# Weight blocks in tiles of a low and a high half, sums stored and loaded as such, and 45 ring tiles

## The chip, the core and the metric

The kernel runs on one core of a Trainium2 chip. The metric is the device time of one execution in microseconds; the time of a version is the median of its runs. The engines are PE (matmuls; PEld is its weight load), DVE (vector work), ACT (activations and casts), POOL and SP (here mostly the issuing of DMAs).

## The reference, cut to what matters

2112 tokens (2048 of a prompt, 64 of a sample) go through one layer with 1024 channels, in fp32:

```python
h = rms_norm(x, g_pre)
vA, bA, cA, zA, q, f, iv, zB, gA, gB = split_cols(h @ w_in)
u = cA * vA
yA = (silu(zA) * bA * causal_conv3(u_ext, conv_w)) @ w_a_out
fg = lb + (1 - lb) * sigmoid(f)
S_new, o = hgrn2_scan(S0, silu(q) * K_B ** -0.5, 1 - fg, iv, log(fg))
o = o * rsqrt(mean(o * o) + EPS)
yB = (o * g_onorm * silu(zB)) @ w_b_out
out = (sigmoid(gA) * yA + sigmoid(gB) * yB) @ w_o
x = x + rms_norm(out, g_post)
gate = sigmoid(rms_norm(x, g_ple) @ w_ple_gate)
x = x + (p @ w_ple_proj) * gate
```

The outputs are x, the last rows of u and the states S_new.

## The kernel before

**Numbers.** A product of fp32 matrices is made of three matmuls: each operand is split into a high half (a cast) and a low half (the rest), and high by high, high by low and low by high are added up in PSUM. A weight block is 128 x 512 (four k of 128); splitting it costs a cast on ACT and a subtraction on DVE (`split`, L207). The low half is kept in DRAM (`lows`, tiles named low), so that a later block of tokens loads it instead.

**Stages.** Three blocks of 768, 704 and 640 tokens go one after the other through these stages: path_b (gates and the eight heads of the scan), path_a (the convolution's products), the merge (W_A, W_B), the output product (W_O), a norm, and the last gate (W_G). A block's norm and the first seven groups of the next block's gates run together.

**sgroup.** The products with w_in run as groups of seven products instead of eight, each of 4 k x 3 matmuls with the width of half a block (384, 352 or 320). Four of the seven take sums or differences of weight blocks (S1 to S4). The first block of tokens makes them (`combined`, `total`) and stores each (DRAM tiles S1 to S4, 256 KB) and its low half (256 KB). Later blocks load both and cast the first (L237). One step of other work is placed behind each product (`hook`; `spread_out` hands out the steps).

**Sums for the other weights.** In the merge of block 1, W_A and W_B run as plain products (`gemm`; the first two j together in `gemm_late`, which takes one k last), while `prepare_sums` makes the sums that blocks 2 and 3 will use (`in_turn`): eight groups of four blocks, loaded on POOL's queue into ring tiles, added and split on ACT and DVE, stored on POOL's queue. It goes on by one group behind W_A's j = 2, 4, 6 and W_B's j = 0, 2, 4, 6, 7. The sums for W_O and W_G are made in path_a of blocks 2 and 3, a whole group behind each j from 3 on.

**Tiles.** Weight blocks go through pools of raw (5), hi (4), lo (4) and s (3) tiles of 2 KB in each partition. Rows of tokens, up to 768 wide, lie in the ring: 47 tiles of one tag. While block 1's W_G runs, 28 of them hold the operands of block 2 and 16 hold W_G's own operand h2. Its results go through ACT (sigmoid) into hf tiles, of which there are nine, and are multiplied by p and added to x; p and x of each j are reloaded into ring tiles on POOL's queue (`reload`, L1107; `final_gate`, L1257 to L1260). Five PSUM banks hold the results of such products.

**Order.** Each engine works through its instructions in the order in which they were laid down; a scheduler lays them down when the program is built. An instruction that waits for a semaphore holds up all behind it on its engine, and a DMA is issued from its engine's queue in the same way.

Of the kernel before, what the change touches and what calls it, by code (L numbers as in the profile page):

```python
# [18 lines left out]
P = 128  # L19
# [4 lines left out]
CH = 64  # L24
# [15 lines left out]
RING = 47  # L40
# [43 lines left out]
def hybrid_step(  # L84
# [56 lines left out]
    def rt(n=None, dt=F32):  # L141
        return ring.tile([P, BMAX + 4], dt, tag="r", name=nm("r"))[:, : n or wide[0]]
# [71 lines left out]

    def load_raw(src):
        raw = wp.tile([P, 4, P], F32, tag="raw", name=nm("raw"), bufs=5)
        SP.dma_start(raw, src)
        return raw

    lows, turn = {}, [0]  # L220

    def low_tile():

        turn[0] += 1
        if turn[0] % 7 in (1, 3, 5):
            return sum_tile(F32R)
        return wp.tile([P, 4, P], F32R, tag="lo", name=nm("lo"))

    def sum_tile(dt=F32):
        return wp.tile([P, 4, P], dt, tag="s", name=nm("s"), bufs=3)  # L230

    def split_w(raw, key=None, queue=SP):

        hi = wp.tile([P, 4, P], F32R, tag="hi", name=nm("hi"))
        if key in lows:
            lo = low_tile()
            A.copy(hi, raw)  # L237
            SP.dma_start(lo.bitcast(F32), lows[key])
            return hi, lo
        lo = wp.tile([P, 4, P], F32R, tag="lo", name=nm("lo"))  # L240
        split(raw, hi, lo)
        if key is not None:
            lows[key] = dram.tile([P, 4, P], F32, tag=f"lo{key}", name=nm("low"), bufs=1)
            queue.dma_start(lows[key], lo.bitcast(F32))
        return hi, lo

    def load_w(idx, anew=False):

        parts = []
        for half_ in range(2):  # L250
            raw = load_raw(w_blk[idx, half_])
            with tc.high_priority():
                unread = W_A <= idx < W_O and (idx % KB < KH or half_ == 0)
                parts.append(split_w(raw, None if anew or unread else (idx, half_)))
# [37 lines left out]
    def keep_sum(name, i1, s, queue):  # L292

        sums.setdefault(i1, {})[name] = dram.tile([P, 4, P], F32, tag=f"{name}_{i1}", name=nm(name), bufs=1)
        queue.dma_start(sums[i1][name], s)
        return split_w(s, (i1, name), queue)

    def kept_w(i1, i2, name, anew=False):

        keys = dict(A11=(i1, 0), A12=(i1, 1), A22=(i2, 1))  # L300
        if name in keys:
            return split_w(load_raw(w_blk[keys[name]]), None if anew else keys[name])
        return split_w(load_raw(sums[i1][name]), (i1, name))

    def combined(i1, i2, first):

        queue = SP if first else G
        with tc.high_priority():
            if not first and i1 in sums:
                return {n: kept_w(i1, i2, n) for _, n, _, _, _ in PRODUCTS}  # L310
            a11, a21, a22, a12 = (load_raw(w_blk[i, h]) for i, h in ((i1, 0), (i2, 0), (i2, 1), (i1, 1)))
# [16 lines left out]
    def prepare_sums(firsts, ahead):  # L328
# [4 lines left out]
        def tile_of(dt=F32):  # L333
            return rt(4 * P, dt).rearrange("p (k c) -> p k c", c=P)

        def load(i1, i2):
            out = [tile_of() for _ in range(4)]
# [4 lines left out]
        def keep(name, i1, s):  # L342
            sums.setdefault(i1, {})[name] = dram.tile([P, 4, P], F32, tag=f"{name}_{i1}", name=nm(name), bufs=1)
            lows[i1, name] = dram.tile([P, 4, P], F32, tag=f"lo{name}_{i1}", name=nm("low"), bufs=1)
# [7 lines left out]
        for n, (i1, _) in enumerate(groups):  # L352
# [15 lines left out]
    def sgroup(i1, i2, hc, sink, first, mid=None, by_k=False):  # L368
# [5 lines left out]
        def product(n, ks):  # L374
# [3 lines left out]
            hi, lo = w[block]  # L378
# [52 lines left out]
    def plain_group(i1, i2, hs, sink, raws=None, between=None):  # L431
# [14 lines left out]
        def add(c, ks):  # L446
            for k in ks:
                hi, lo = w[c, k // KH]
# [1082 lines left out]
```

## Time and profile before

| | us |
|---|---|
| median of 3 runs (2616.1 to 2618.68) | 2617.19 |
| profiled execution | 2618.3 |
| its span | 2616.6 |
| PE busy | 2584.3 |
| DVE busy | 1648.8 |
| ACT busy | 1525.9 |
| POOL busy | 376.6 |
| loads of raw tiles from S, 256 KB each | 408 |

The span is the time from the first to the last instruction in the profile. Busy times count matmuls, vector and activation work, not the issuing of DMAs or waits. A group's row gives its busy time, the mean of one instruction in ns, the idle time of its engine just before, and what ended that time. The DMA list gives for each kind of transfer its number, its size and the median time from issue to landing.

### The profile page before, as it was taken

Reading aid. Unit: us, or ns where it says so; the run is one execution under the profiler, and the core shown is the slowest. Engines: PE = TensorE matmul, PEld = TensorE weight load, DVE = VectorE, ACT = ScalarE, POOL = GpSimd, SP = SyncE. Lnnn points to the kernel's source line nnn. Section 1 sums busy time; section 2 is a strip of 40 time slices with the busy share of each in tenths; the row PEclk is TensorE's granted clock in tenths of the full one; section 3 lists DMA queues with packets and bytes.
Section 4 is the critical chain, followed back from the end, with each engine's and each line's share of the span. In section 5 each row is a group of like instructions: output and inputs, shape, how many; then the busy total and the mean of one; then the engine's idle time right before and its main releaser. Section 6 shows DMA issues by size and latency. Waiting matters only on the chain.

```text
span 2616.6 us, 47076 instructions
## 1 busy us (share of the span) xinstructions
PE 2584.3 (99%) x16432; PEld 2564.4 (98%) x16432; DVE 1648.8 (63%) x3165; ACT 1525.9 (58%) x2908; POOL 376.6 (14%) x698
## 2 busy tenths in 40 slices
PE   8999999999999999999999999999999999999999
PEld 8999999999999999999999999999999999999999
DVE  8687788788757655445554557845344444568776
ACT  6666576554433564567775546546677755556746
POOL 1000000110144021210011221002100000211110
PEclk9999999999999999999999999999999999999999
DMA  7677677788788698876768998859977779999977
GB/s 274 220 262 265 232 247 263 274 302 268 267 330 286 233 379 284 279 242 223 229 224 296 364 381 304 305 167 377 366 252 244 245 254 332 381 335 359 344 264 264
DMA packets 362095, 747.01 MB, mean 285 GB/s; under 512 B 44513, under 2 KB 49153, under 8 KB 361857
## 3 DMA queue, kind: packets, MB, share of 16 engines
q1 hardware_dynamic: 319680, 579.81, 64.2%
q0 software_dynamic: 41888, 164.15, 17.2%
q8 instruction: 129, 2.11, 0.3%
q14 instruction: 110, 0.89, 0.1%
q10 hardware_dynamic: 288, 0.05, 0.0%
HBM read 532.26 MB, written 211.57 MB: 284 GB/s over the span
## 4 chain that ended last, share of the span: by engine, by line
PE 82%; DMA 5%; ACT 4%; DVE 3%; issue 2%; POOL 1%; ACTq 0%; POOLq 0%; SPq 0%; DVEq 0%
PE pg L382 16%; PE pg L383 16%; PE pg L384 16%; PE pg L551 5%; PE pg L550 5%; PE pg L549 5%; PE pg L516 4%; PE pg L517 4%; PE pg L518 3%; DMA raw<-S 2%; DMA r<-w_blk 1%; PE pa L984 1%; PE pa L1020 1%; PE pa L970 1%; ACT hi L237 1%
## 5 line engine op out<-in xcount | busy, mean ns | idle before, releaser
L382 PE MATMUL pg<-r,hi 128*128 128x320 f32 (+2 forms) x3304 | 1087.5, 329 | 5.5 <-DVE r L429 3.8
L383 PE MATMUL pg<-r,hi 128*128 128x320 f32 (+2 forms) x3304 | 1069.3, 324 | 0.0
L384 PE MATMUL pg<-r,lo 128*128 128x384 f32 (+2 forms) x2356 | 766.9, 326 | 4.1 <-DMA lo<-low 4.1
L237 ACT CAST hi<-raw 128x512 fp32r<-128x512 f32 x720 | 442.9, 619 | 465.5 <-PE pg L383 137.2
L382 PEld LDWEIGHTS pg<-r,hi 128*128 128x128 f32 x3304 | 622.6, 188 | 7.9 <-issue 4.7
L383 PEld LDWEIGHTS pg<-r,hi 128*128 128x128 f32 x3304 | 622.7, 188 | 0.2 <-DVE r L207 0.2
L384 PEld LDWEIGHTS pg<-r,lo 128*128 128x128 f32 x2356 | 443.2, 188 | 5.1 <-DMA lo<-low 5.1
L384 PE MATMUL pg<-r,s 128*128 128x352 f32 (+1 forms) x948 | 299.3, 316 | 1.0 <-DMA s<-low 1.0
L549 PE MATMUL pg<-r,hi 128*128 128x384 f32 (+1 forms) x768 | 256.1, 334 | 1.6 <-ACT r L207 1.6
L550 PE MATMUL pg<-r,hi 128*128 128x384 f32 (+1 forms) x768 | 256.1, 334 | 0.1
L207 ACT CAST hi<-raw 128x512 fp32r<-128x512 f32 x218 | 134.7, 620 | 178.2 <-PE pg L550 57.9
L207 DVE TENSOR_TENSOR r<-r,r 128x320 fp32r<-128x320 f32 (+7 forms) x298 | 182.0, 633 | 64.9 <-ACT r L207 63.9
L551 PE MATMUL pg<-r,lo 128*128 128x384 f32 (+1 forms) x656 | 219.9, 335 | 0.0
L517 PE MATMUL pg<-r,hi 128*128 128x320 f32 (+1 forms) x672 | 211.1, 316 | 0.2 <-DVE r L207 0.2
L516 PE MATMUL pg<-r,hi 128*128 128x320 f32 (+1 forms) x672 | 206.0, 316 | 0.9 <-ACT r L207 0.8
L207 DVE TENSOR_TENSOR lo<-raw,hi 128x512 fp32r<-128x512 f32 x218 | 149.3, 686 | 63.1 <-ACT hi L207 60.4
L207 ACT CAST r<-r 128x320 fp32r<-128x320 f32 (+7 forms) x298 | 161.0, 576 | 46.0 <-DVE r L715 12.7
L207 ACT CAST hi<-s 128x512 fp32r<-128x512 f32 x160 | 98.0, 618 | 145.7 <-PE pg L383 130.8
L384 PEld LDWEIGHTS pg<-r,s 128*128 128x128 f32 x948 | 178.5, 188 | 1.8 <-DMA s<-low 1.8
L396 ACT COPY hf<-pg 128x352 f32<-128x352 f32 (+2 forms) x354 | 156.7, 444 | 3.8 <-PE pg L384 3.6
L207 DVE TENSOR_TENSOR lo<-s,hi 128x512 fp32r<-128x512 f32 x160 | 110.1, 689 | 68.9 <-ACT hi L207 67.3
L549 PEld LDWEIGHTS pg<-r,hi 128*128 128x128 f32 x768 | 144.8, 189 | 2.2 <-ACT r L207 2.2
(365 smaller groups left out, 4097.7 us busy)
## 6 DMA issues: line engine op xcount, KB each, us to landing
raw<-w_blk SPq DMA_DIRECT2D x570, 256.0 KB, 4.2
lo<-low SPq DMA_DIRECT2D x411, 256.0 KB, 4.6
raw<-S SPq DMA_DIRECT2D x408, 256.0 KB, 4.4
low<-lo SPq DMA_DIRECT2D x314, 256.0 KB, 3.5
s<-low SPq DMA_DIRECT2D x309, 256.0 KB, 4.5
S<-s SPq DMA_DIRECT2D x152, 256.0 KB, 3.2
r<-w_blk POOLq DMA_DIRECT2D x64, 256.0 KB, 6.8
S<-r POOLq DMA_DIRECT2D x64, 256.0 KB, 5.8
```

Source lines behind the costliest of these rows:

```text
L207: return A.copy(hi, src).ins, V.tensor_tensor(lo, src, hi.bitcast(F32), ALU.subtract).ins
L237: A.copy(hi, raw)
L382: add(hi[:, k, :], xhi, start=start and k == 0, stop=False)
L383: add(hi[:, k, :], xlo, start=False, stop=False)
L384: last[0] = add(lo[:, k, :], xhi, start=False, stop=k == KH - 1).ins
L396: copied = A.copy(got[n], ps[bank])
L516: add(hi[:, k, :], xhi, start=start and k == 0, stop=False)
L517: add(hi[:, k, :], xlo, start=False, stop=False)
L518: last[0] = add(lo[:, k, :], xhi, start=False, stop=k == KH - 1).ins
L549: T.matmul(ps, hi[:, k % 4, :], xhi[:, c], start=k == ks[0], stop=False)
L550: T.matmul(ps, hi[:, k % 4, :], xlo[:, c], start=False, stop=False)
L551: last[0] = T.matmul(ps, lo[:, k % 4, :], xhi[:, c], start=False, stop=k == ks[-1]).ins
```

## The change

- A weight block lies in one tile of two halves, low first (tag w, 7 of them), which takes the place of the hi and lo tiles and, for loaded sums, of the raw tile.
- A sum is stored as one such tile (512 KB) and loaded as one, with no cast. Raw weight blocks are still loaded, cast, and completed by a load of the low half.
- The raw tag has 6 tiles, and its tiles also take the sums of the first block and, in `prepare_sums` during the merge of block 1, the high and low halves of each sum: eight to a group, where four s tiles held the low halves.
- `prepare_sums` makes S3 before S1. For W_O and W_G each group is cut into four pieces, placed behind the products of path_a's groups by way of hooks.
- `gemm_late` goes through the k in a circle behind the late one: from 4 on for block 2's W_O.
- The last block's heads get one empty hook more, the norm's plan has one step more before each spread of the root mean squares.
- The ring has 45 tiles of 768 + 2 columns instead of 47 of 768 + 4; the small tags qc, one and ms have one tile less each.

```diff
-RING = 47
+RING = 45
+WEIGHTS = 7
+RAWS = 6
...
-        return ring.tile([P, BMAX + 4], dt, tag="r", name=nm("r"))[:, : n or wide[0]]
+        return ring.tile([P, BMAX + 2], dt, tag="r", name=nm("r"))[:, : n or wide[0]]
...
+    def raw_tile(dt=F32):
+        return wp.tile([P, 4, P], dt, tag="raw", name=nm("raw"), bufs=RAWS)
+
+    def both():
+        return wp.tile([P, 2, 4, P], F32R, tag="w", name=nm("w"), bufs=WEIGHTS)
...
+    def get_w(src, key=None):
+        raw = load_raw(src)
+        if key not in lows:
+            return split_w(raw, key)
+        t = both()
+        A.copy(t[:, 1], raw)
+        SP.dma_start(t[:, 0].bitcast(F32), lows[key])
+        return t
...
     def kept_w(i1, i2, name, anew=False):
         keys = dict(A11=(i1, 0), A12=(i1, 1), A22=(i2, 1))
         if name in keys:
-            return split_w(load_raw(w_blk[keys[name]]), None if anew else keys[name])
-        return split_w(load_raw(sums[i1][name]), (i1, name))
+            return get_w(w_blk[keys[name]], None if anew else keys[name])
+        t = both()
+        SP.dma_start(t.bitcast(F32), sums[i1][name])
+        return t
...
             def total(name, x, y, op):
-                s = sum_tile()
+                s = raw_tile()
                 V.tensor_tensor(s, x, y, op)
-                out[name] = keep_sum(name, i1, s, queue)
+                out[name] = split_w(s)
+                queue.dma_start(sum_home(name, i1), out[name].bitcast(F32))
                 return s
...
         def keep(name, i1, s):
-            G.dma_start(sums[i1][name], s)
-            lo = sum_tile(F32R) if ahead else tile_of(F32R)
-            split(s, lo, lo)
-            G.dma_start(lows[i1, name], lo.bitcast(F32))
+            home = sum_home(name, i1)
+            hi, lo = (raw_tile(F32R) if ahead else blocks_of(F32R) for _ in range(2))
+            split(s, hi, lo)
+            G.dma_start(home[:, 1], hi.bitcast(F32))
+            G.dma_start(home[:, 0], lo.bitcast(F32))
...
             V.tensor_tensor(a22, a21, a22, ALU.add)
-            keep("S1", i1, a22)
             V.tensor_tensor(a21, a11, a21, ALU.subtract)
+            if not ahead:
+                yield
             keep("S3", i1, a21)
             V.tensor_tensor(a11, a22, a11, ALU.subtract)
+            if not ahead:
+                yield
+            keep("S1", i1, a22)
+            V.tensor_tensor(a12, a12, a11, ALU.subtract)
+            if not ahead:
+                yield
             keep("S2", i1, a11)
-            V.tensor_tensor(a12, a12, a11, ALU.subtract)
             keep("S4", i1, a12)
...
-        ks = [k for k in range(KB) if k != late] + [late]
+        ks = [(late + 1 + k) % KB for k in range(KB)]
...
-            hooks.extend([None] * 3 if first and hd == 0 else [])
+            hooks.extend([None] * (3 if first and hd == 0 else int(bl["last"] and len(attn) == 2)))
...
-                if j >= 3:
+                if j == 3:
                     next(sums_, None)
+                elif j > 3 and not first:
+                    hooks.extend([partial(next, sums_, None), None, None] * 4)
...
-            spread_out((norm, (0, 1, 0, 1) + (0, 1, 0) * KB + (0, 1, 0, 1) + (0, 1) * KB))
+            spread_out((norm, (0, 1, 0, 0, 1) + (0, 1, 0) * (KB - 1) + (0, 1) + (0, 1, 0, 0, 1) + (0, 1) * KB))
```

Three places of the built order. First DVE in the merge of block 1, behind W_B's j = 2. Its two result banks are pg_2345 and pg_2346 before, pg_1897 and pg_1898 now; the r tiles are the group's blocks and sums, the s and raw tiles the low halves of S1 (before) and S3 (now). Before:

```order
L356 TENSOR_TENSOR r_2322_9424<-r_2321_9423,r_2322_9424 128x512 [waits DMASW1_49,DMASW0_49]
L358 TENSOR_TENSOR r_2321_9423<-r_2320_9422,r_2321_9423 128x512 [waits DMASW7_49,DMASW3_49,DVE_49]
L207 TENSOR_TENSOR lo_2382_9662<-raw_2380_9659,hi_2381_9661 128x512 [waits DMAHW5_49,PE_49,Activation_49]
L1139 TENSOR_TENSOR r_2336_9462<-pg_2345_9483,r_2336_9462 128x384 [waits DMASW3_49]
L1139 TENSOR_TENSOR r_2336_9462<-pg_2346_9508,r_2336_9462 128x384
L207 TENSOR_TENSOR s_2356_9554<-r_2322_9424,s_2356_9554 128x512 [waits DMASW2_49,Activation_49]
```

Now:

```order
L359 TENSOR_TENSOR r_1876_8826<-r_1875_8825,r_1876_8826 128x512 [waits DMASW1_49,DMASW0_49]
L360 TENSOR_TENSOR r_1875_8825<-r_1874_8824,r_1875_8825 128x512 [waits DMASW7_49,DVE_49]
L1148 TENSOR_TENSOR r_1890_8864<-pg_1897_8883,r_1890_8864 128x384 [waits DMASW3_49,PE_49]
L1148 TENSOR_TENSOR r_1890_8864<-pg_1898_8908,r_1890_8864 128x384 [waits PE_49]
L209 TENSOR_TENSOR raw_1908_8954<-r_1875_8825,raw_1907_8953 128x512 [waits DMASW4_49,Activation_49]
```

The first low half of the group stands behind the product's two result banks in both. What moved is its tile: it was an s tile, it is a raw tile now.

Second SP's queue at the same place, with the loads of the raw tiles for W_B's j = 3 (raw_2366 and raw_2369 before, raw_1918 and raw_1920 now). Before:

```order
L217 DMA raw_2366_9582<-w_blk 128x512 [waits DMAHW3_49,DVE_49]
L217 DMA raw_2369_9588<-w_blk 128x512 [waits DMAHW5_49,DVE_49]
L217 DMA raw_2377_9653<-w_blk 128x512 [waits DMAHW6_49,DMAHW4_49,DVE_49]
L217 DMA raw_2380_9659<-w_blk 128x512 [waits DMAHW0_49,DVE_49]
L217 DMA raw_2405_9766<-w_blk 128x512 [waits DMAHW1_49,DVE_49]
```

Now:

```order
L226 DMA raw_1895_8878<-w_blk 128x512 [waits DMASW6_49,DMAHW1_49,DMASW2_49,DVE_49]
L226 DMA raw_1918_8982<-w_blk 128x512 [waits DMAHW2_49,DMASW7_49,DMAHW5_49,DMASW4_49,DVE_49]
L226 DMA raw_1920_8987<-w_blk 128x512 [waits DMASW5_49,DMASW4_49,DVE_49]
L226 DMA raw_1927_9051<-w_blk 128x512 [waits DMAHW4_49,DMAHW2_49,DVE_49]
L226 DMA raw_1929_9056<-w_blk 128x512 [waits DMAHW6_49,DMASW6_49,DMASW5_49]
```

DMASW semaphores belong to POOL's DMAs, DMAHW to SP's. The loads waited for SP's own DMAs and for DVE; now they wait for DMAs of POOL as well. DMASW7 at raw_1918 is the store of raw_1908, the tile whose place it takes.

Third POOL's queue at block 1's W_G, with the reloads of p and x for j = 0 and 1 (r_2903, r_2904, r_2915, r_2918 before; r_2352, r_2353, r_2362, r_2365 now). Before:

```order
L1107 DMA r_2903_11978<-p_32_175 128x768 [waits DMASW7_49,DMASW3_49,DVE_49]
L1107 DMA r_2904_11980<-x_2802_11593 128x768 [waits DMASW4_49,DMASW1_49]
L1107 DMA r_2915_12048<-p_39_203 128x768 [waits DMASW5_49,DMASW2_49]
L1260 DMA y_fm<-r_2903_11978 128x768 [waits DMASW6_49,DVE_49]
L1107 DMA r_2918_12058<-x_2834_11679 128x768 [waits DMASW4_49]
L1107 DMA r_2929_12126<-p_46_231 128x768 [waits DMASW6_49,DMASW0_49]
```

Now, from the reload of x of j = 0 on (that of p stands six rows ahead and waits for no matmul):

```order
L1116 DMA r_2353_11221<-x_2274_10887 128x768 [waits DMASW1_49,PE_49]
L1116 DMA r_2362_11287<-p_39_203 128x768 [waits PE_49]
L1116 DMA r_2365_11297<-x_2296_10954 128x768 [waits DMASW3_49,PE_49]
L237 DMA low_2468_11871<-w_2467_11868 128x512 [waits DMASW4_49,DVE_49]
L1269 DMA y_fm<-r_2352_11219 128x768 [waits DMASW5_49,DVE_49]
L321 DMA S4_2471_11878<-w_2470_11875 128x1024 [waits DMASW6_49,DVE_49]
L1116 DMA r_2374_11363<-p_46_231 128x768 [waits DMASW7_49,PE_49]
L1269 DMA y_fm<-r_2362_11287 128x768 [waits DMASW0_49,DVE_49]
```

The reloads waited for other DMAs and for DVE. Now all but the first wait for PE: the tiles that they go into are those of W_G's operand, and r_2353 takes the place of a tile that the last of the sixteen products reads.

More of the change, by code (lines that the diff above doesn't have):

```diff
@@ L250, in load_w @@
         for half_ in range(2):
[L251 removed]
             with tc.high_priority():
                 unread = W_A <= idx < W_O and (idx % KB < KH or half_ == 0)
[L254 removed]
+                parts.append(get_w(w_blk[idx, half_], None if anew or unread else (idx, half_)))
         return parts
@@ L290, in hybrid_step, with sum_home @@
     sums = {}
[L292 to L296, printed above, removed]
+    def sum_home(name, i1):
+        home = dram.tile([P, 2, 4, P], F32, tag=f"{name}_{i1}", name=nm(name), bufs=1)
+        sums.setdefault(i1, {})[name] = home
+        return home
     def kept_w(i1, i2, name, anew=False):
@@ L310, in combined @@
                 return {n: kept_w(i1, i2, n) for _, n, _, _, _ in PRODUCTS}
+            queue = SP if first else G
             a11, a21, a22, a12 = (load_raw(w_blk[i, h]) for i, h in ((i1, 0), (i2, 0), (i2, 1), (i1, 1)))
@@ L936, in tile3 @@
             if nt == 1:
-                return small.tile([P, 1, P], F32, tag="one", name=nm("one"), bufs=5)
+                return small.tile([P, 1, P], F32, tag="one", name=nm("one"), bufs=4)
             return cols3(rt(nt * P), nt)
```

54 lines of the change are left out of this document (19 added, 35 removed).

## The prediction

> **What bounds the kernel now.** First the page's busy times, then the windows of 100 us, then what the matmul engine (PE) waits for, last the prices of the steps that the change puts in a chain.
>
> ```profile
> PE 2584.3 (99%) x16432; PEld 2564.4 (98%) x16432; DVE 1648.8 (63%) x3165; ACT 1525.9 (58%) x2908; POOL 376.6 (14%) x698
> ```
>
> PE is the bound: 2616.6 us of span less 2584.3 leave 32.3 us of idle time. Everything that the change takes from ACT lies under PE. So only two things count: which of these 32.3 us go, and which new ones come.
>
> ```profile
> 0.00:100.00 100.00, 91.10 (x510) 88.65 (x511) 76.71 (x139) 64.44 (x117) 14.06 (x29) 1.00 0.73 261
> 900.00:1000.00 100.00, 97.21 (x603) 95.49 (x602) 56.72 (x86) 63.45 (x116) 18.80 (x32) 1.00 0.96 349
> 1800.00:1900.00 100.00, 97.59 (x662) 96.82 (x660) 40.13 (x74) 63.10 (x118) 14.68 (x26) 0.98 1.01 377
> 2200.00:2300.00 100.00, 95.55 (x635) 94.38 (x635) 51.83 (x89) 50.62 (x101) 22.93 (x47) 0.98 1.02 379
> 750.00:800.00 50.00, 50.00 (x288) 50.00 (x287) 29.13 (x46) 14.91 (x25) 14.06 (x27) 1.00 0.67 243
> 1050.00:1100.00 50.00, 50.00 (x301) 50.00 (x300) 23.02 (x41) 24.85 (x42) 10.26 (x19) 1.00 0.77 272
> ```
>
> Columns: window, sum, PE, weight loads, DVE, ACT, POOL, PE clock, DMA share, GB/s. The first 100 us (8.9 idle) are not touched. Losses stand where DMA is full (0.96 to 1.02). The last two rows are the ones to keep: the merge of block 1 (W_A, W_B) and the end of its W_G have no idle time at all, and the change rebuilds the buffers just there.
>
> ```profile
> PE pg L384 <- DMA lo<-low: 4.1, 3, 2.2
> PE pg L382 <- DVE r L429: 3.8, 4, 1.8
> PE pa L953 <- DVE r L429: 2.0, 7, 0.3
> PE pa L624 <- POOL cols L613: 1.8, 6, 0.5
> PE pg L549 <- ACT r L207: 1.6, 2, 1.2
> PE pg L518 <- DMA lo<-low: 1.0, 1, 1.0
> PE pg L384 <- DMA s<-low: 1.0, 2, 0.5
> L382 PE MATMUL pg<-r,hi 128*128 128x320 f32 (+2 forms) x3304 | 1087.5, 329 | 5.5 <-DVE r L429 3.8 <-ACT hf L396 0.9 <-ACT hi L237 0.7
> 1701.50:1704.90 3.40, 3.40 (x13) 3.15 (x12) 2.56 (x6) 0.98 (x2) 0.00 (x0) 0.50 0.11 42
> 1803.90:1807.30 3.40, 3.40 (x15) 3.40 (x14) 1.83 (x3) 2.90 (x5) 0.54 (x1) 0.50 1.04 414
> ```
>
> The waits (total us, times, longest) give 15.3 us, L382's two smaller ones 1.6. The last two rows are the clock after W_O's stall and after one at 1803: 0.50 for 3.4 us, so 1.7 us more each. With a third in the window from 2200 (its mean clock is 0.98, too) that makes 5.1. At stake: 15.3 + 1.6 + 5.1 = 22.0 us.
>
> **What it removes.** 408 casts of loaded sums go from ACT:
>
> ```profile
> L237 ACT CAST hi<-raw 128x512 fp32r<-128x512 f32 x720 | 442.9, 619 | 465.5 <-PE pg L383 137.2 <-issue 66.0 <-DMA raw<-S 54.1
> L356 DVE TENSOR_TENSOR r<-r,r 128x512 f32<-128x512 f32 x16 | 11.0, 690 | 53.2 <-DMA r<-w_blk 53.2
> ```
>
> 408 x 0.619 = 252 us of ACT work, worth on PE only the 0.7 behind L237 and what ACT held up. Term by term: W_O of block 2 starts at k=4 with weights ahead, so its 1.6 and its dip of 1.7 go. The seven transposes (L953) get one more product between them and DVE: 2.0 goes. The pieces take L356's wait for a block (53.2 us on 10 occasions) out of the way of bank c's sum (L429): of L382's 5.5 I take 4.6, and one dip of 1.7. The bytes stay the same, in half as many loads, so of the 6.1 of waits for low halves I take 3.5, and half a dip, 0.9. Of L624's 1.8 the extra hook takes 0.8. Sum: 1.6 + 1.7 + 2.0 + 4.6 + 1.7 + 3.5 + 0.9 + 0.8 = 16.8. Bounds: 22.0 if all goes; 8.0 if only W_O (3.3), the transposes (2.0) and half of L382 (2.7) do.
>
> **What it adds in the merge of block 1.** The high and low halves of each prepared sum now lie in the raw tiles, which the weights are loaded into. A weight load must wait until a sum's store has landed, and that sum's split stands on DVE behind L1148 (L1139 before), which needs the matmuls just done (the DVE rows in the section on the change). W_B's j=3 (the rows shown), its j=7 and W_O begin behind such a chain, and nothing else is queued on PE. Prices:
>
> ```profile
> raw<-w_blk SPq DMA_DIRECT2D x570, 256.0 KB, 4.2
> S<-s SPq DMA_DIRECT2D x152, 256.0 KB, 3.2
> S<-r POOLq DMA_DIRECT2D x64, 256.0 KB, 5.8
> low<-lo POOLq DMA_DIRECT2D x8, 256.0 KB, 4.0
> raw<-w_ple SPq DMA_DIRECT2D x8, 128.0 KB, 2.8
> r<-w_blk POOLq DMA_DIRECT2D x64, 256.0 KB, 6.8
> L1139 DVE TENSOR_TENSOR r<-pg,r 128x384 f32<-128x384 f32 x16 | 8.7, 552 | 2.5 <-DMA r<-g__1389_5594 1.6 <-PE pg L551 0.9
> L207 DVE TENSOR_TENSOR lo<-raw,hi 128x512 fp32r<-128x512 f32 x218 | 149.3, 686 | 63.1 <-ACT hi L207 60.4 <-DMA low<-lo 1.2 <-ACT r L207 0.9
> L207 ACT CAST hi<-raw 128x512 fp32r<-128x512 f32 x218 | 134.7, 620 | 178.2 <-PE pg L550 57.9 <-PE pg L383 47.9 <-issue 38.3
> 1059.69 0.34 PE L549 MATMUL pg<-r,hi 128*128 128x384 f32 x1
> 1060.21 0.34 PE L549 MATMUL pg<-r,hi 128*128 128x384 f32 x1
> ```
>
> The chain at j=3: 0.55 (L1139) + 0.69 (sum's low) + a store from POOL of 4.9 (between 4.0 and 5.8) + a load of 4.2 + a cast of 0.62 + part of the next split, 0.35, + five hand-overs of some 0.1 = 11.8, taken as 11.5. Bounds: 8 with landings of 3.2 and 2.8, 14 with a store of 5.8 and a load that shares the queue with four block loads (6.8). Queued behind on SP are the three other weight loads of j=3 and j=4, and W_O's chain is the same: 11.5 (8 to 14). At j=7 the split waits for j=5's end, and j=6 covers 48 matmuls of 0.175 (0.52 for three, last two rows) = 8.4: 11.7 - 8.4 = 3.3 (0 to 5.6). At W_A's j=3 the store is queued on POOL behind eight loads, not behind PE: 2 (0 to 6).
>
> [...]
>
> **What 45 ring tiles add.** While W_G of block 1 runs, the next block's operands hold 28 tiles and h2 holds 16: 44. Of 47, three were left for the reloads of p and x; of 45, one is. So x of j=0, p and x of j=1 (the POOL rows in the section on the change) wait until the last of W_G's 16 gemms gives back h2's tiles. ACT can take nine results into hf tiles and two more from j=0's, the last five stay in PSUM, and path_b's first bank needs one of them.
>
> ```profile
> r<-p POOLq DMA_DIRECT2D x8, 384.0 KB, 5.3
> r<-x POOLq DMA_DIRECT2D x8, 384.0 KB, 5.6
> L1258 DVE TENSOR_TENSOR r<-r,hf 128x384 f32<-128x384 f32 (+1 forms) x32 | 17.2, 538 | 36.9 <-DMA r<-p 24.4 <-ACT hf L1257 12.3
> L1259 DVE TENSOR_TENSOR r<-r,r 128x768 f32<-128x768 f32 (+1 forms) x16 | 14.8, 922 | 0.3
> L1257 ACT ACTIVATE hf<-pg 128x384 f32<-128x384 f32 (+1 forms) x32 | 15.2, 475 | 40.6 <-PE pg L551 40.6
> 1085.08 0.33 PE L383 MATMUL pg<-r,hi 128*128 128x352 f32 x1
> 1085.57 0.32 PE L383 MATMUL pg<-r,hi 128*128 128x352 f32 x1
> ```
>
> From the last gemm's start: x issued at 0.2, landed at 5.8; add 0.9, product with the gate 0.55, sigmoid 0.5: 7.8 us. The gemm lasts 24 x 0.175 = 4.2, so PE waits 3.6. The third bank needs p of j=2, issued on POOL behind the store of y (6.7) and a sum's store (8.2): 8.7 + 5.3 + 0.55 + 0.5 = 15.0, and PE is there after two products of 12 x 0.163 at 11.7: 3.3. Together 6.9 (2 to 10). Later the first head's preparation stands ahead of a bank's sum on DVE, about twelve instructions with ACT between: 3 x 0.92 + 9 x 0.54 = 7.6, against two products of cover, 3.9: 4 (0 to 9).
>
> **Clock.** After such stalls PE ran at 0.50 for 3.4 us. For six places I take five dips: 8.5 (2 to 8 of them: 3.4 to 13.6). [...]
>
> **Sum.** Losses 11.5 + 3.3 + 11.5 + 2 + 6.9 + 4 + 8.5 = 47.7 (bounds 21.4 to 72). The profiled execution took 2618.3 us, 1.7 more than its span and 1.1 more than the median of 2617.19. 2618.3 - 16.8 + 47.7 = 2649.2, against the median 2648.
>
> **Rivals.**
>
> *Only the weights' chains stall.* The reloads of p and x have been fast enough before (L1258 waits 24.4 us for p and PE never does), and the hf tiles take up the rest. Then 11.5 + 3.3 + 11.5 + 3 dips (5.1) = 31.4, less 16.8: 2632. Against it: before, three tiles rotated through all of W_G; with one there is no reload until its end.
>
> *Not slower: short landings.* Place: the two chains at W_B's j=3 and at W_O. With SP waiting, DMA is nearly empty there, and landings are short: 3.2 for a store, 2.8 for a load, 8 us a chain; j=7 is covered, the ring costs 2, three dips 5.1: 23.1. If all 22.0 at stake goes too, the time is 2618. It decides once a chain falls below 8.5 us. For it: the DMA share of 0.67 in the merge. Against it: the chain holds two landings in a row and no row of this size is under 3. [...]
>
> *The gain does not come.* Bytes are unchanged and the windows with losses run at a DMA share of about 1, so the waits for low halves and DVE's waits for blocks stay: 8.0 instead of 16.8, and landings at the upper rows make the two chains 14 each: 2648 + 8.8 + 5.0 = 2662.
>
> **How the numbers follow.** Forecast 0.52, only the chains 0.20, no gain 0.19, short landings 0.09. A measurement of this kernel tells 0.2% (5.2 us) from no change. Short landings split into 0.04 within that and 0.05 faster, when they are shorter still; the other three are slower: 0.91. The range takes in the chains alone (2632) and no gain (2662) with some 5 us for the bounds of the landings: 2628 to 2668. The forecast's own range is 2638 to 2660.
>
> **What would show it.** In the merge of block 1, matmuls of line 559 with idle times of 8 to 14 us behind ACT's cast or DVE's split of a weight tile, twice, and one of 2 to 6; on SP, loads of raw tiles that wait for stores of S. After W_G, line 391 idle 2 to 5 us twice behind ACT's sigmoid (L1266), and DVE waiting for p and x at L1267 and L1268. A granted clock of 0.50 behind each. On the gain's side: no idle time ahead of the transposes, none ahead of W_O in block 2, less than 1 us behind the sums of bank c, 2.6 us left of waits for low halves. I am wrong if the windows from 700 to 1150 us stay full, or if blocks 2 and 3 do not lose their 16.8 us.

## The result, and the profile after

The changed kernel takes 2675.73 us (median of 4 runs, 2673.2 to 2679.12), the kernel before 2616.64 us (4 runs, 2613.66 to 2618.68). The ratio is 1.0228 [1.021, 1.0245]: 59 us slower, where 31 had been predicted. The profiled execution took 2673.2 us; the prediction's sum for it was 2649.2.

First the page of the changed kernel, span and busy times.

```profile
span 2671.5 us, 45400 instructions
PE 2593.1 (97%) x16432; PEld 2571.0 (96%) x16432; DVE 1653.2 (62%) x3171; ACT 1307.2 (49%) x2500; POOL 374.4 (14%) x696
```

ACT has lost 218.7 us of work, and the time has gone the other way. PE idles 2671.5 - 2593.1 = 78.4 us, where it idled 32.3 before. The windows of the changed kernel say where (columns as in the prediction):

```profile
700.00:900.00 200.00, 174.33 (x952) 170.30 (x951) 111.93 (x170) 60.82 (x101) 62.05 (x116) 0.94 0.72 255
1000.00:1200.00 200.00, 177.04 (x1052) 174.14 (x1051) 84.96 (x143) 74.02 (x135) 28.02 (x50) 0.96 0.72 248
2300.00:2400.00 100.00, 93.26 (x618) 92.01 (x617) 60.32 (x113) 39.09 (x82) 23.58 (x48) 0.98 0.97 369
```

The same two stretches of 200 us in the kernel before:

```profile
700.00:900.00 200.00, 200.00 (x1148) 199.96 (x1147) 136.71 (x208) 79.61 (x129) 64.26 (x120) 1.00 0.79 282
1000.00:1200.00 200.00, 200.00 (x1264) 199.48 (x1263) 96.70 (x192) 107.40 (x199) 31.46 (x56) 1.00 0.77 260
```

The merge of block 1 and its W_O (700 to 900) idle for 25.7 us, W_G with the first heads behind it (1000 to 1200) for 23.0. Both were full. All the rest idles for 29.7 us instead of 32.3. What PE waits for in the changed kernel, in the rows that bear on the change (total us, times, longest; its third longest, 7.0 at L1093, stood there before, too, as 6.9 at L1084):

```profile
PE pg L559 <- ACT w L209: 24.8, 6, 10.4
PE pg L391 <- DVE hf L431: 12.1, 2, 11.0
PE pg L391 <- ACT hf L405: 6.0, 7, 1.9
PE pg L391 <- ACT hf L1266: 5.1, 2, 3.1
PE pg L391 <- DMA w<-S: 4.5, 5, 2.9
PE pg L560 <- DVE r L209: 3.4, 1, 3.4
PE pg L393 <- DMA w<-low: 1.3, 1, 1.3
```

The first row is the weights of the merge, the second almost wholly one wait of 11 us for the first head. Gone are the waits ahead of the transposes and of block 2's W_O.

The clock, of which a stretch at 0.50 is called a dip: the three long ones in the two places, as windows of their own (the clock is the first number behind POOL's). Two short ones, at 851.9 and 1114.7, have 3.41 us of PE each. Half of PE's time in them is counted as lost, an estimate from the recorded 0.50: (3.22 + 5.90 + 3.41) / 2 = 6.3 us in the merge, (4.88 + 3.41) / 2 = 4.1 behind it. Blocks 2 and 3 lose 1.7 (one stretch of 3.4 us) instead of 5.1. The matmuls themselves slow down by somewhat less: those of 128x384 start 0.32 us apart in the dip at 865.5 and 0.175 us apart ahead of it, those of 128x352 0.293 us apart at 1114.9 and 0.161 at 1125.1, a factor of 1.8. By it the losses would be 5.7 and 3.7 us.

```profile
804.10:814.34 10.24, 3.22 (x10) 2.99 (x11) 6.60 (x10) 1.89 (x4) 4.81 (x10) 0.50 0.93 328
865.50:875.74 10.24, 5.90 (x18) 5.68 (x19) 3.03 (x5) 2.21 (x5) 4.06 (x8) 0.50 0.96 321
1155.70:1169.35 13.65, 4.88 (x17) 4.88 (x18) 9.61 (x19) 5.77 (x10) 1.08 (x2) 0.50 0.54 192
```

**The chain ahead of W_B's j = 3**, followed in the timeline of the changed kernel (start, duration, engine, what; in brackets the idle time before it):

```profile
800.72 0.56 DVE L1148 TENSOR_TENSOR r<-pg,r 128x384 f32<-128x384 f32 x1 [2.38 <-PE pg L561]
801.20 0.68 DVE L209 TENSOR_TENSOR raw<-r,raw 128x512 fp32r<-128x512 f32 x1
...
802.18 0.54 POOL L351 DMA_DIRECT2D S<-raw  x1 [2.28 <-DVE raw L209]
802.71 1.60 POOL L343 DMA_DIRECT2D r<-w_blk  x3
...
804.61 7.54 SPq L226 DMA_DIRECT2D raw<-w_blk  x3
...
810.45 0.62 ACT L209 CAST w<-raw 128x512 fp32r<-128x512 f32 x1 [4.33 <-DMA raw<-w_blk]
...
811.12 0.69 PE L559 MATMUL pg<-r,w 128*128 128x384 f32 x1 [10.44 <-ACT w L209]
```

It is the chain that was predicted, link by link: the result bank's multiplication, the low half of the sum, its store from POOL, and when that has landed the load on SP, the cast, the matmul. Only its two DMAs share the time otherwise: the store landed within 2.4 us (802.18 to 804.61), the load took 5.8 (804.61 to 810.45), beside the four block loads that POOL had issued from 802.71 on. SP's own waits show how general it is. The changed kernel has

```profile
SPq L226 <- DMA S<-raw: 121.0, 24, 31.1
```

and the kernel before waited once at its line (L217) for a store of S, for 0.9 us.

**The first head**, DVE and PE of the changed kernel:

```profile
1149.69 0.52 DVE L411 TENSOR_TENSOR hf<-hf,pg 128x352 f32<-128x352 f32 x1
1156.65 0.96 DVE L1268 TENSOR_TENSOR r<-r,r 128x768 f32<-128x768 f32 x1 [6.44 <-DMA r<-x]
...
1163.90 0.52 DVE L431 TENSOR_TENSOR hf<-hf,pg 128x352 f32<-128x352 f32 x1
...
1164.47 0.66 PE L391 MATMUL pg<-r,w 128*128 128x352 f32 x1 [10.96 <-DVE hf L431]
```

DVE stands still for 6.4 us at an x of the last gate: POOL had issued its reload only at 1149.0, and it landed 7.5 us later. The reload of p before it was issued at 1136.8; in between stand five stores of weight tiles on POOL's queue (S and low), four of which waited for DVE's low halves of these tiles. The head's preparation is queued behind that, and behind the preparation the sum of the bank (L431) that PE needs.

### The profile page after: what moved, and what is told of

The parts are those of the page before. It is cut to its first block, busy times and chain, and to the rows that moved or that the text cites. A ratio compares the mean times of both kernels' runs of the same rounds, so it can differ in the third digit from the quotient of the medians.

```text
span 2671.5 us, 45400 instructions
## 1 busy us (share of the span) xinstructions
PE 2593.1 (97%) x16432; PEld 2571.0 (96%) x16432; DVE 1653.2 (62%) x3171; ACT 1307.2 (49%) x2500; POOL 374.4 (14%) x696
## 5 line engine op out<-in xcount | busy, mean ns | idle before, releaser
L391 PE MATMUL pg<-r,w 128*128 128x320 f32 (+2 forms) x3304 | 1090.8, 330 | 29.7 <-DVE hf L431 12.1
L393 PE MATMUL pg<-r,w 128*128 128x320 f32 (+2 forms) x3304 | 1069.9, 324 | 1.3 <-DMA w<-low 1.3
L392 PE MATMUL pg<-r,w 128*128 128x320 f32 (+2 forms) x3304 | 1068.1, 323 | 0.0
L391 PEld LDWEIGHTS pg<-r,w 128*128 128x128 f32 x3304 | 623.1, 189 | 36.5 <-DVE hf L431 12.7
L392 PEld LDWEIGHTS pg<-r,w 128*128 128x128 f32 x3304 | 624.5, 189 | 0.1
L393 PEld LDWEIGHTS pg<-r,w 128*128 128x128 f32 x3304 | 622.3, 188 | 2.1 <-DMA w<-low 2.1
L209 ACT CAST w<-raw 128x512 fp32r<-128x512 f32 x384 | 236.5, 620 | 295.6 <-PE pg L393 119.7
L209 DVE TENSOR_TENSOR w<-raw,w 128x512 fp32r<-128x512 f32 x384 | 263.5, 689 | 143.7 <-ACT w L209 135.6
L246 ACT CAST w<-raw 128x512 fp32r<-128x512 f32 x306 | 189.0, 619 | 281.7 <-PE pg L393 153.2
L559 PE MATMUL pg<-r,w 128*128 128x384 f32 (+1 forms) x768 | 258.3, 337 | 26.0 <-ACT w L209 24.8
L560 PE MATMUL pg<-r,w 128*128 128x384 f32 (+1 forms) x768 | 257.9, 336 | 3.4 <-DVE r L209 3.4
L561 PE MATMUL pg<-r,w 128*128 128x384 f32 (+1 forms) x768 | 257.1, 336 | 0.9 <-DVE w L209 0.5
L527 PE MATMUL pg<-r,w 128*128 128x320 f32 (+1 forms) x672 | 211.3, 316 | 0.0
L528 PE MATMUL pg<-r,w 128*128 128x320 f32 (+1 forms) x672 | 209.9, 314 | 0.0
L526 PE MATMUL pg<-r,w 128*128 128x320 f32 (+1 forms) x672 | 207.8, 315 | 0.7 <-DMA w<-S 0.7
L559 PEld LDWEIGHTS pg<-r,w 128*128 128x128 f32 x768 | 146.1, 190 | 28.8 <-ACT w L209 27.0
L560 PEld LDWEIGHTS pg<-r,w 128*128 128x128 f32 x768 | 146.0, 190 | 3.9 <-DVE r L209 3.9
L561 PEld LDWEIGHTS pg<-r,w 128*128 128x128 f32 x768 | 145.8, 190 | 2.7 <-DVE w L209 2.6
L527 PEld LDWEIGHTS pg<-r,w 128*128 128x128 f32 x672 | 126.2, 188 | 2.2 <-DVE r L209 1.6
```

Source lines behind the costliest of these rows:

```text
L209: return A.copy(hi, src).ins, V.tensor_tensor(lo, src, hi.bitcast(F32), ALU.subtract).ins
L246: A.copy(t[:, 1], raw)
L391: add(hi[:, k, :], xhi, start=start and k == 0, stop=False)
L392: add(hi[:, k, :], xlo, start=False, stop=False)
L393: last[0] = add(lo[:, k, :], xhi, start=False, stop=k == KH - 1).ins
L526: add(hi[:, k, :], xhi, start=start and k == 0, stop=False)
```

## The experiments

Theory 1: a sum's halves in the raw tiles make the weights of the merge wait for stores. Theory 2: 45 ring tiles make W_G and the first heads wait. Beside them: whether the pieces gain anything, and what is left for the tiles of two halves. A time without a number of runs is one execution; the kernel before ranged from 2611.55 to 2618.87 over 25 runs, so that single executions tell only some 8 us apart.

**Sums in tiles of their own (the changed kernel).**

```diff
-WEIGHTS = 7
-RAWS = 6
+WEIGHTS = 6
+RAWS = 4
+SUMS = 4
...
-                s = raw_tile()
+                s = sum_tile()
...
-            hi, lo = (raw_tile(F32R) if ahead else blocks_of(F32R) for _ in range(2))
+            hi, lo = (sum_tile(F32R) if ahead else blocks_of(F32R) for _ in range(2))
```

> The changed kernel, but sums and the prepared high and low halves get four tiles of their own (tag s), raw has 4, w has 6 (the same memory), the ring keeps 45. Theory 1 (a weight load waits for the landing of a sum's store because both use the raw tag): the waits of line 559 behind the weight cast in the merge of block 1 (25.7 us between 730 and 870 us, and some 6 us of half clock) go almost wholly, the stalls from 1048 to 1165 us (26 us) stay: about 2645 us. Rival (the merge is slow because two operations in a chain on DVE came late, whatever the tiles): the merge keeps more than 15 us, time above 2660.

2663.95 us (before on that chip 2614.36). Its windows:

```profile
700.00:900.00 200.00, 200.00 (x1145) 199.97 (x1144) 135.13 (x208) 78.22 (x132) 67.64 (x127) 1.00 0.84 294
1000.00:1200.00 200.00, 178.21 (x1065) 175.22 (x1064) 88.36 (x158) 80.10 (x146) 27.50 (x50) 0.97 0.69 234
```

The merge is full again, the second place hardly changed (21.8 idle). So the stalls of the merge come from the shared tiles. The time fell by 12 us only. Other waits came in: those for w<-S go from 4.5 to 12.2 us. That one w and two raw tiles fewer bring them is likely, but was not tried by itself. The run shows the place, not the price.

**Eight raw tiles, still shared (the changed kernel).**

```diff
-WEIGHTS = 7
-RAWS = 6
+WEIGHTS = 6
+RAWS = 8
```

> The changed kernel with 8 raw tiles instead of 6 and 6 w tiles instead of 7 (the same memory as the run with own tiles), raw tiles still shared by weights and prepared sums. Theory 1: sharing as such is the cause, so the two long waits ahead of W_B's j=3 and W_O stay near 10 and 7 us; the merge keeps 15 us or more. Rival (six raw tiles were only too few): the merge's waits fall below 5 us, as with own tiles.

2674.04 us. The merge idles 20.6 us (179.36 of 200 busy), and SP still waits 93.9 us for S<-raw. Two more tiles do not end it. Together with the run before this says that it is the sharing. The second place idles 13.0 us here (187.01 busy) instead of 23.0, of which more below.

**A ring of 47 tiles (the changed kernel),** with two w tiles fewer to make the room.

```diff
-RING = 45
-WEIGHTS = 7
+RING = 47
+WEIGHTS = 5
```

> The changed kernel with the ring back at 47 tiles, paid for by 5 w tiles instead of 7; raw tiles still shared. Theory 2 (45 ring tiles leave one tile for the reloads in W_G of block 1): the waits at 1048 (W_G's start), 1114, 1123, 1138, 1147 and 1164 us, 23 us with some 4 us of half clock, go to under 3 us; the merge keeps its 25 us: about 2648 us, more if 5 w tiles are too few. Rival (the 11 us behind DVE L431 at 1164 come from the new order of pieces and hooks): these 11 us stay, about 2660.

2711.82 us. Windows, and the first row of PE's waits:

```profile
700.00:900.00 200.00, 172.73 (x936) 169.93 (x934) 112.97 (x172) 60.31 (x100) 62.06 (x116) 0.93 0.70 251
1000.00:1200.00 200.00, 200.00 (x1247) 199.76 (x1247) 103.42 (x182) 92.58 (x170) 32.26 (x58) 1.00 0.83 282
```

```profile
PE pg L391 <- DMA w<-S: 28.1, 21, 3.9
```

The mirror of the first run: the second place is full, the 11 us at the first head are gone, and the merge stalls as without the edit. The loss is another: with five w tiles the loaded sums come too late in blocks 2 and 3.

**Both (the changed kernel).** As in the first run, with three tiles for sums, and the ring of 47.

```diff
-RING = 45
-WEIGHTS = 7
-RAWS = 6
+RING = 47
+WEIGHTS = 4
+RAWS = 5
+SUMS = 3
```

> Both: own tiles for sums (3), raw 5, w 4, ring 47, which is the memory of the kernel before; kept from the change are the tiles of two halves, the loads of 512 KB, the pieces, the k order and the hooks. Theory 1 and 2 together: no wait over 1 us between 700 and 1200 us, and 2605 to 2620 us, about the time before or below it. If something else in the change costs time (fewer tiles ahead of a hand-over, the pieces), the waits behind loads of w in blocks 2 and 3 grow, and it is above 2620.

2759.22 us. Both places are all but full (195.59 and 199.62 of 200), and the loads of sums now hold PE up all over blocks 2 and 3 (w<-S: 49.6 us on L395, 36.6 on L530). A tile of two halves takes the room of two tiles for its whole life, and four are too few. In these runs, each kind of tile was paid for with another; seven w tiles with own tiles for sums and 47 ring tiles were not tried.

**The price of each part, alone in the kernel before.** First the ring, and nothing else.

```diff
-RING = 47
+RING = 45
```

> The kernel before with 45 ring tiles instead of 47 and nothing else. Theory 2 (the ring alone makes the stalls around the end of W_G in block 1): PE's waits between 1000 and 1120 us rise from 0 to between 15 and 28 us behind the sigmoids (L1257), h2's splits and the drains of the first heads, with two or three stretches of half clock: 2635 to 2648. Rival (they need the changed order or the larger weight tiles): below 2622.

2642.17 us, against 2616.14 for the kernel before on that chip: +26.0. Its windows:

```profile
1000.00:1100.00 100.00, 93.34 (x521) 92.08 (x520) 33.23 (x50) 29.33 (x54) 14.46 (x27) 0.97 0.62 209
1100.00:1200.00 100.00, 89.49 (x570) 88.28 (x569) 49.73 (x106) 60.90 (x111) 14.62 (x25) 0.93 0.75 251
```

17.2 us idle, and stretches at half clock in which PE was busy for 15.9, so 7.9 lost by the same estimate: 25.1 of the 26.0 are found here. The longest stalls are 4.2 us for a load of a low half, 4.0 at the first head, and 2.5 and 1.9 behind the sigmoids.

Then the low halves of the prepared sums in the five raw tiles instead of the s tiles:

```diff
-            lo = sum_tile(F32R) if ahead else tile_of(F32R)
+            lo = wp.tile([P, 4, P], F32R, tag="raw", name=nm("raw"), bufs=5) if ahead else tile_of(F32R)
```

> The kernel before with one edit: in the merge of block 1 the low halves of the prepared sums lie in raw tiles (the five that the weights are loaded into) instead of the three s tiles. Theory 1 says this alone makes PE wait for the chain of split, store, load and cast ahead of W_B's j=3 and of W_O: 15 to 30 us of waits of L549 between 700 and 870 us, and 2635 to 2655. Rival (the new tile kind, the store of the high half or fewer casts are needed for it): below 5 us and about 2617.

2641.02 us against 2616.58: +24.4.

```profile
700.00:900.00 200.00, 183.10 (x998) 179.07 (x997) 120.05 (x182) 67.18 (x110) 63.09 (x118) 0.96 0.75 260
1000.00:1200.00 200.00, 200.00 (x1252) 199.81 (x1251) 99.77 (x179) 107.53 (x198) 32.11 (x58) 1.00 0.82 273
```

16.9 idle and 7.3 by the clock, estimated in the same way, make 24.2. Each part brings its own stall to its own place and none to the other: for the places and the prices both theories hold. The way is another than theory 1 has it. Ahead of j = 3, PE waits 4.7 us here for a cast on ACT at 802.25, and the load of the block that it casts had been issued at 787.44, 14.8 us earlier. The cast stands on ACT behind those of the sums, and these behind one that waits for DVE's result of j = 2. SP waits 53.5 us for stores of raw tiles in this run (low<-raw), but the wait of PE ahead of j = 3 does not end with a load.

**The gains, alone in the kernel before.** The order of k, the empty hook and the norm's plan, without the pieces:

```diff
-        ks = [k for k in range(KB) if k != late] + [late]
+        ks = [(late + 1 + k) % KB for k in range(KB)]
...
-            hooks.extend([None] * 3 if first and hd == 0 else [])
+            hooks.extend([None] * (3 if first and hd == 0 else int(bl["last"] and len(attn) == 2)))
...
-            spread_out((norm, (0, 1, 0, 1) + (0, 1, 0) * KB + (0, 1, 0, 1) + (0, 1) * KB))
+            spread_out((norm, (0, 1, 0, 0, 1) + (0, 1, 0) * (KB - 1) + (0, 1) + (0, 1, 0, 0, 1) + (0, 1) * KB))
```

> The kernel before with the k in a circle, the extra hook at the last block's heads and the norm's new plan, without the pieces. Expected gain: 2.0 of transposes and about 1 at the spreads; the k order alone, without the seven w tiles, has its weights no earlier, so that the wait ahead of W_O (1.6 and 1.7 of clock) goes only if it hung on the last operands of the first k: 2610 to 2614, and 2609 if W_O's wait goes, too.

2609.16 us (10 runs), ratio 0.9975 [0.9965, 0.9984].

The same with the pieces as in the change (sums for W_O and W_G cut in four, three hooks apart):

```diff
+            if not ahead:
+                yield
...
-                if j >= 3:
+                if j == 3:
                     next(sums_, None)
+                elif j > 3 and not first:
+                    hooks.extend([partial(next, sums_, None), None, None] * 4)
```

> The kernel before (its tiles, its ring of 47) with only the parts of the change that move work: sums for W_O and W_G in four pieces placed as in the change, the k in a circle, one hook more at the last block's heads, the norm's new plan. If these parts bring what the changed kernel shows for them (1.7 of wait and 1.7 of clock ahead of W_O, 2.0 ahead of the transposes, some 1 at the spreads), and the pieces as in the changed kernel gain nothing (DVE waits for the blocks still, now ahead of L431's counterpart), the time is 2608 to 2611 against 2616. If the pieces do take the 4.6 us that the prediction gave them, it is about 2605.

2611.76 us (10 runs), ratio 0.9984 [0.9974, 0.9993]. And with the pieces two hooks apart:

```diff
-                    hooks.extend([partial(next, sums_, None), None, None] * 4)
+                    hooks.extend([partial(next, sums_, None), None] * 4)
```

> As the run before, with the four pieces two products apart instead of three, so that a group's blocks are loaded eight products (about 14 us) ahead of their first use instead of five (about 9 us). If the pieces' remaining stall is DVE waiting for blocks loaded too late, the waits of PE in path_a of blocks 2 and 3 (before 3.8 us behind L429's sum, and in the changed kernel as much behind the copy L405) fall below 2 us, and the time is 2 to 4 us under the run with pieces three products apart. If the load's lead does not matter, both are within 1 us.

2609.75 us (10 runs), ratio 0.9976 [0.9966, 0.9985].

The small edits bring 7.0 us, and the pieces nothing on top of them: with them it is 2.6 us slower three apart and 0.6 two apart, and the intervals overlap. PE's waits for bank c and what is behind it, in the first and in the second of these three kernels:

```profile
PE pg L382 <- DVE r L429: 3.2, 3, 1.7
```

```profile
PE pg L392 <- ACT hf L406: 1.9, 4, 0.9
```

The sum of bank c (L429) no longer ends a wait, but ACT's copies do in its place. DVE still waits 56.1 us for the first block of each group (55.9 without the pieces). Cutting up the work behind this wait does not touch it. Two hooks apart, where the blocks are asked for earlier, it falls to 45.5.

**Everything but the tiles of two halves.** The kernel with the pieces three hooks apart, with the ring of 45 and the low halves in raw tiles.

```diff
-RING = 47
+RING = 45
...
-            lo = sum_tile(F32R) if ahead else tile_of(F32R)
+            lo = wp.tile([P, 4, P], F32R, tag="raw", name=nm("raw"), bufs=5) if ahead else tile_of(F32R)
```

> Everything of the change except the tiles of two halves: the kernel before with its pieces, hooks, order of k and norm plan, a ring of 45 tiles, and the prepared low halves of block 1's merge in the raw tiles (five of them). Alone these measured about -4 (pieces, hooks and k), +26 (45 ring tiles) and +24 us (low halves in raw tiles). Additive theory: the parts add up to 2617 - 4 + 26 + 24 = about 2662, and the 13 us left up to the changed kernel's 2675 belong to the tiles of two halves (eight raw tiles to a group instead of four, sums loaded as one 512 KB transfer). Rival, interaction: the stalls of merge and ring delay each other (the ring's prepared sums come later, more half clock), so that this kernel takes 2670 to 2680 and the tiles of two halves cost nothing. Second rival: overlap, the two stalls share what they wait for, 2645 to 2655.

2659.74 us against 2618.59: +41.2, where the parts alone add up to 26.0 + 24.4 - 4.4 = 46.0. They add up within what single executions tell, and nothing shows that the stalls feed each other. Its windows:

```profile
700.00:900.00 200.00, 183.24 (x995) 178.76 (x995) 118.39 (x180) 67.17 (x110) 62.00 (x116) 0.95 0.74 259
1000.00:1200.00 200.00, 181.48 (x1076) 178.29 (x1075) 86.74 (x152) 92.20 (x164) 29.14 (x53) 0.97 0.72 246
```

The changed kernel's profiled execution is 13.5 us longer than this one: 8.9 more idle in the merge, 4.4 more behind it. W_B's j = 3 shows the first of these. In this kernel

```profile
803.70 0.83 ACT L207 CAST r<-r 128x768 fp32r<-128x768 f32 x1 [2.43 <-DVE r L1150]
804.44 1.26 ACT L207 CAST raw<-r 128x512 fp32r<-128x512 f32 x2
805.60 0.61 ACT L207 CAST hi<-raw 128x512 fp32r<-128x512 f32 x1
806.27 0.69 PE L559 MATMUL pg<-r,hi 128*128 128x384 f32 x1 [5.37 <-ACT hi L207]
```

j = 3's first block had been loaded at 793.73, and only the second waited for its tile, until 804.34. PE waits 5.4 us for the cast of the first, which stands on ACT behind the sums' casts, as in the run with the shared raw tiles alone. In the changed kernel a group takes eight raw tiles, the first block has to wait for a store as well, and PE waits 10.4. There it is the chain of two landings that was predicted. That eight tiles to a group make the rest of the 13.5 too was not tried by itself.

Behind the merge the first head shows what a late x costs. With the eight raw tiles of the run above, x is on time and PE waits 4.8 us there. With the ring of 45 alone DVE stands 2.9 us at x, and PE waits 4.0 and, for a low half that stands behind x on DVE, 2.3. In this kernel DVE stands 2.6, and PE waits 3.3 and 4.0. In the changed kernel DVE stands 6.4, and PE waits 11.0. With eight raw tiles the reload of x is issued right behind that of p, so how late it comes depends on what the order of POOL's queue puts ahead of it.

**A version that gains.** Since DVE waits for blocks, the kernel with the small edits was given each group's blocks one group ahead, in path_a as in the merge:

```diff
-            if ahead and n + 1 < len(groups):
+            if n + 1 < len(groups):
...
-            if not ahead and n + 1 < len(groups):
-                nxt = load(*groups[n + 1])
```

> The kernel before with the k in a circle, the hooks and the norm's plan, sums for W_O and W_G whole as before, but each group's four blocks are loaded one group ahead (four more ring tiles in path_a of blocks 2 and 3, where the ring of 47 has them free). If DVE's wait for blocks that were asked for too late is what makes PE wait behind L429's sums in path_a, these waits (2.6 us around 2280 and 0.6 at 1547 with the late loads) and DVE's wait at L356 (53 us) fall below 1 us and 10 us: 2605 to 2607 against 2609 without the lead. If the stall is the four additions of DVE in one piece, the waits stay at 2 to 3 us and the time at 2609.

2607.72 us (5 runs), ratio 0.9964 [0.995, 0.9978]. With the pieces two hooks apart as well:

> The same with the lead of one group and the four pieces two products apart. If the late loads alone were the cause, it is as fast as the run with whole groups and a lead, within 1 us; if the pieces matter as well, it is 1 to 3 us faster.

2606.68 us (5 runs), ratio 0.9966 [0.9952, 0.9979]. DVE's row for the first sum of a group, with the load ahead and no pieces:

```profile
L356 DVE TENSOR_TENSOR r<-r,r 128x512 f32<-128x512 f32 x16 | 11.0, 687 | 22.4 <-DMA r<-w_blk 22.4
```

22.4 us of waiting instead of 53.2 before and 55.9 with the small edits alone, though not below the 10 that were expected, and no wait of PE for bank c's sum is left. Both beat the kernel before and the changed one; they can't be told from each other, nor from the small edits alone (2609.16 on another chip). So the earlier load is shown in the waits and not in the time.

## Why the prediction was right or wrong

Against the profiled executions (2618.3 and 2673.2, a difference of 54.9), idle time and clock together:

| | predicted us | measured us |
|---|---|---|
| merge of block 1 and W_O | 28.3 + 5.1 clock (three dips) | 25.7 + 6.3 clock |
| W_G and first heads | 10.9 + 3.4 clock (two dips) | 23.0 + 4.1 clock |
| gains elsewhere | 12.5 + 4.3 clock | 2.6 + 3.4 clock |
| sum | +30.9 | +53.1 |

- **What bounds the kernel: right.** PE, and only its waits counted. The 218.7 us less on ACT took away the 0.7 that PE had waited for such a cast (L237), and nothing else of it shows.
- **The chains in the merge: right in mechanism and in their sum, less so one by one.** j = 3 took 12.0 (10.4 and 1.5 at its next block) for 11.5, j = 7 3.3 for 3.3, W_A 3.0 for 2, W_O 7.4 for 11.5, below its lower bound of 8. W_O's store landed in 2.3 us and its load in 3.4; there no block loads were ahead of it. The link that was mis-sized is the store, 4.9 taken and 2.3 measured. At j = 3 the load made up for it, 5.8 for 4.2, so that this number came out close is in part luck. The two stores from POOL took 2.3 us each, the loads on SP 3.4 and, beside four others, 5.8. The five hand-overs of some 0.1 us were the author's estimate; ahead of j = 3 DVE's low half and POOL's store of it lie 0.3 us apart (801.88 to 802.18), the cast and the matmul 0.05 (811.07 to 811.12).
- **The ring: right in mechanism, too small by more than half.** W_G's end took 2.0 + 3.1 = 5.1 for 6.9. The step that failed is the first head: 4 (0 to 9) was worked out from DVE's own twelve instructions against two products of cover, and it measured 11.0. Left out was that x of the last gate is late there as well, 6.4 us of DVE standing still ahead of those instructions. With x on time the head costs 4.8, as the run with eight raw tiles shows. And one place was missing: at the start of W_G, h2's last low halves need ring tiles that come free only when a spill (a store of a tile of gates, g) has landed. DVE waits 6.2 us for it, PE 3.4 and, at the next low halves, 1.2:

```profile
1047.17 0.96 DVE L209 TENSOR_TENSOR r<-r,r 128x768 fp32r<-128x768 f32 x1 [6.24 <-DMA g__2350_11215<-r]
...
1048.19 0.44 PE L560 MATMUL pg<-r,w 128*128 128x384 f32 x1 [3.38 <-DVE r L209]
```

  The prediction counted the tiles at W_G's end (44 of 45) and not on the way there. Two smaller stalls, of 1.2 and 1.1 us, follow at 1138 and 1147.
- **The gains: the step that failed is what the pieces and the loads of sums would bring.** W_O's wait and its dip, 3.3, and the transposes, 2.0, came as said. The 6.3 of bank c did not: where L382 had waited 3.8 for DVE's sum, L391 now waits 6.0 for ACT's copies. At one place in path_a of block 3, DVE's and ACT's rows:

```profile
2309.90 0.69 DVE L359 TENSOR_TENSOR r<-r,r 128x512 f32<-128x512 f32 x1 [6.70 <-DMA r<-w_blk]
...
2311.25 0.48 DVE L431 TENSOR_TENSOR hf<-hf,pg 128x320 f32<-128x320 f32 x1
...
2311.76 0.47 ACT L845 ACTIVATE r<-hf 128x320 f32<-128x320 f32 x1 [8.39 <-DVE hf L431]
...
2312.95 0.42 ACT L405 COPY hf<-pg 128x320 f32<-128x320 f32 x1
```

  The sum of the bank (L431) still stands behind the wait for a group's block, ACT behind the sum, and the copy that PE needs behind that; PE lost 1.9 us here. The pieces moved DVE's wait for blocks (53.2 before, 60.5 now) and did not shorten it. Nor did the waits for low halves shrink: 6.1 in all before, and 1.3 for low halves with 5.2 for sums now. The rival of no gain had named this, from the same bytes at a DMA share of about 1; what was wrong was to set it against the forecast, since it could come on top of it, and did.
- **The clock: right in number.** Five dips came, and five were predicted; counted at half they cost 10.4 us for 8.5, since three of them last 10 to 14 us instead of 3.4. The 1.7 us that the prediction takes for a dip of 3.4 us is the same estimate; by the factor of 1.8 it would be 1.5.
- **The range: too low.** It ended at 2668, with the gains' lower bound and some 5 us for the landings. The bounds of the terms themselves (losses of 72, gains of 8.0) reach to 2682, and a chain of 5.8 and 6.8 us adds up to 15.3, not to the 14 that was taken as its upper bound. Outside of their bounds on the slow side were the head (11.0 for at most 9), the places that were not listed (4.6 at W_G's start, 2.3 behind its end), 8.9 together, and the gains (6.0 for at least 8.0), 2.0 more; the median lies 7.7 above the range. The direction and the two places were right.

What stays open: the remaining 1.8 us between 53.1 and 54.9 (2.5 if the clock is taken at the factor of 1.8), which lie in PE's busy time, and how the 13.5 us of the tiles of two halves divide between eight raw tiles to a group, the loads of 512 KB and the order of the queues.

## What to carry to other kernels

Before two uses are put into one pool of tiles, ask what frees a tile in each: a tile that a store frees makes the next load wait for a landing (121.0 us of waits on SP here, 93.9 with two raw tiles more), and if that store's data come from late work, two landings stand on the path (2.3 and 5.8 us ahead of j = 3). Count a ring's tiles at the point where they are fewest and along the way there (two tiles fewer alone cost 26.0 us), and follow each late reload down the in-order queue of the engine that waits for it: what stands behind it can cost more than the reload (DVE stood still for 6.4 us at x, PE waited 11.0). When a pool is shared, look at the order on the in-order engines as well as at the landings: a cast can stand behind others long after its block was asked for (14.8 us with the low halves in raw tiles alone). Work taken from an engine that is not the bound paid next to nothing here (218.7 us of ACT, 0.7 of PE's waits), and the wait for a late operand was shortened by an earlier load (55.9 to 22.4 us) and not by cutting up the work that waits for it (56.1).

## What the runs showed of the hardware

Between the first 13 and the last 7 us of the changed kernel's profile the granted clock is 0.50 in six stretches and 1.00 everywhere else. The stretches begin at 804.08, 851.86, 865.52, 1114.69, 1155.65 and 2336.66 us and last 10.24, 3.41, 10.24, 3.41, 13.65 and 3.41 us. These lengths are 3, 1 and 4 times 3.413 us, and from one start to the next it is 14, 4, 73, 12 and 346 times as much. Windows of 3.41 us around the fourth:

```profile
1111.28:1114.69 3.41, 1.40 (x9) 1.07 (x8) 2.81 (x5) 1.11 (x2) 1.79 (x4) 1.00 0.92 297
1114.69:1118.10 3.41, 3.41 (x14) 3.41 (x13) 0.96 (x1) 0.82 (x2) 2.03 (x5) 0.50 0.99 379
1118.10:1121.52 3.42, 1.78 (x11) 1.48 (x10) 0.00 (x0) 0.29 (x1) 1.52 (x3) 1.00 0.98 346
1121.52:1124.93 3.41, 1.99 (x12) 1.99 (x13) 1.33 (x3) 0.96 (x2) 0.00 (x0) 1.00 1.02 402
1124.93:1128.35 3.42, 3.42 (x23) 3.24 (x22) 2.92 (x5) 0.93 (x2) 1.07 (x2) 1.00 1.01 399
```

Here the longer of two stalls is the one without a half clock behind it. That of 2.0 us lies in one window (1.40 of 3.41 busy), and the next window is at 0.50; that of 3.07 us falls half into one window and half into the next (1.78 and 1.99 busy), and the clock stays at 1.00. In the 3.41 us ahead of the six stretches PE idles for 3.40, 3.13, 3.06, 2.01, 2.14 and 2.86 us, and ahead of the three of the kernel before (1701.49, 1803.89 and 2295.41) for 1.72, 2.08 and 1.84. What brings the half clock about was not shown beyond that.
